# Fewer dense and more listed up blocks in two PEER layers, an earlier end of gate placing, and one gate product per pair of blocks on GpSimd

## The chip, the cores and the metric

The kernel runs on one core of a Trainium2 chip. The engines are TensorE (PE; its weight loads are shown apart as PEld), VectorE (DVE), ScalarE (ACT), GpSimd (POOL) and the queue that issues most DMAs (SP). The metric is the device time of one execution in microseconds; less is better. A difference of 0.2% (some 3 us) is about what a measurement of this kernel can tell from none.

## The reference, cut to what matters

Two layers, each an attention mixer followed by a PEER expert mixer, over 256 tokens of width 1024 in float32. The change touches the PEER mixers alone:

```python
expert = jnp.take_along_axis(cand_idx, pos, axis=-1)   # 8 heads x 16 experts of 16384 for each token
gate = jax.nn.softmax(best, axis=-1)
u = w_down[e_blk]
a = jnp.einsum('td,ted->te', x_blk, u)
hg = jax.nn.gelu(a, approximate=False) * g_blk
y = jnp.einsum('te,ted->td', hg, w_up[e_blk])
```

A token picks 128 of 16384 experts, and y is the sum of their up rows, weighted by gelu times gate.

## The kernel before, in words

**Arithmetic.** A float32 operand is split into two float16 parts, high and low, and a product is three matmuls: high by high, high by low, low by high (`mm3`, `proj`, `rows`; all are issued at L480).

**The weight stream.** All weights pass through one `Stream`, in blocks of 128 x 1024 float32 (512 KB). SP loads a block into one of 6 `raw` buffers (L212), ACT writes the high part `hi` (L152), DVE the low part `lo` (L161); 6 buffers each of `hi` and `lo` lie between them and PE. Each engine works through its instructions in a fixed order, so what stands behind a waiting instruction waits too.

**The down stage of a PEER layer.** The 16384 experts are laid out as 128 blocks of 128 rows. The activation of every expert for every token is computed: 128 down blocks, taken in 64 pairs, 48 matmuls `d` of 128x256 for a pair (loop at L1576). The gelu goes to `A`, an area of the `arena` with 256 columns (the tokens) for each block (L1587, L1589).

**Placing the gates.** Once the experts are chosen, their gates are placed, in 64 groups of 4 tokens. For a group, `prepare` makes a one-hot matrix `hot` on DVE (L1392), the product `gate` of one-hot and gate, on DVE in the kernel before (L1394), and a second part of `gate` on ACT (four instructions, L1400). A pair of blocks later `place` runs on PE, behind the pair's `d`: eight matmuls `G` and four matmuls `seen` for a group. `G` is then copied by ACT to the blocks of `A` that have not been computed (L1419) and multiplied by DVE into those that have (L1421); a pair that is computed later has its gelu multiplied in by DVE (L1590). Four buffers hold `hot` and `gate`, three PSUM banks hold `G`. How many groups a pair prepares (`want`, L1597) is what is left, shared over the pairs until `END` blocks ahead of the stage's end, and rounded up:

```python
left = max(1, (NKEYS - (END if short else 4) - b0) // 2)
want = min(64 - groups, -(-(64 - groups) // left))
```

With END = 6 and placing begun at block 58, the pairs prepare 1, 2, 3 and then 2 groups each, 32 pairs in all; the last group is placed behind blocks 122 and 123.

**What `seen` is for.** `seen` tells, for each expert outside of the dense blocks, whether a token of the first half (128 tokens) or of the second picks it. From it `lists` (L1424 on) makes, for each of the 128 partitions, a list of the blocks that it needs: JB entries for both halves, JO for each half alone, and what does not fit there is spread over a tail of TB entries. This is a generator: each `list_on(1)` lets it emit one step, three steps per pair at the end of the down stage and one per up item. Its steps for the tail need small matmuls `moved` (L1513), 16 for each 8 columns of ROWTAIL.

**The table.** In DRAM lies a `table` for each layer, with one row for each expert outside of the dense blocks: its up row, copied there block by block during earlier stages (L217), and its 256 activations, stored from `A` by SP in three parts of the tokens as they are complete (`store`, L1545).

**The up stage.** `ITEMS` sets the order: first the DENSE up blocks, which are loaded straight from the input, then the listed blocks, each a gather of 128 table rows by a GpSimd DMA (L208) into one of 9 places that lie over the last blocks of `A`. A block for both halves takes 12 matmuls `y` of 128x512, a block for one half takes 6. `xh` and `xl` are the split activations of an item, `hi` and `lo` its split weights. A gather may start only when all stores and copies into the table have landed.

**A flag.** If the lists do not hold all that the tokens need, the program computes everything again without lists.

Of the kernel before, what the change touches and what calls it, by code (L numbers as in the profile page):

```python
# [65 lines left out]
LEAST, MOST, ROW, SMALL = 64.0, 2.0 ** 40, 4.0, 2.0 ** -24  # L66
BOTH, MOSTLY = 128, 1120
CHECKS = 7 * P
DENSE, HEAD = 20, 20
RARE = P - DENSE  # L70
JB, JO, TB, ROWTAIL = 32, 24, 16, 32
BOTHS = JB + TB
WIDE = D + T
PARTS = (0, 128), (128, 192), (192, 256)
FETCHED, DEEP = 9, 8
LISTED = BOTHS + 2 * JO
END = 6
CHUNKED = 4
TO_PE, FROM_PE, TAIL_READY = 3, 4, 42

# [254 lines left out]
def tile_trunk(ctx: ExitStack, tc: tile.TileContext, ins, out: bass.AP, short, shared):  # L335
    nc = tc.nc
# [19 lines left out]
    def ps(name):  # L356
        return psp.tile([P, 512], F32, tag="ps", name=name)
# [115 lines left out]
    def dve(emit):  # L473
        return link("dve", emit)
# [16 lines left out]
    def proj(o, blk, w=P, late=False):  # L491

        h, l = blk
        if late:
            for c in range(NC):
                mm(o, h[:, c * w : (c + 1) * w], xh[:, c, :], c == 0, False)
                mm(o, h[:, c * w : (c + 1) * w], xl[:, c, :], False, False)
            for c in range(NC):
                ins = mm(o, l[:, c * w : (c + 1) * w], xh[:, c, :], False, c == NC - 1)
            return ins  # L500
        for c in range(NC):
            s = slice(c * w, (c + 1) * w)
            ins = mm3(o, (h[:, s], l[:, s]), (xh[:, c, :], xl[:, c, :]), c == 0, c == NC - 1)
        return ins
# [690 lines left out]
    def peer(li):  # L1195
# [165 lines left out]
        def spend(income):  # L1361

            purse[0] += income
            while purse[0] > 0:
                cost = next(bg, None)
                if cost is None:
                    return True
                purse[0] -= cost
            return False
# [15 lines left out]
        def prepare(g4, engine):  # L1385
            hot = ohp.tile([P, 2, P, 4], F16, tag="V", name="hot")
            gate = ohp.tile([P, 2, 4, P], F16, tag="U", name="gate")
            four = slice(4 * g4, 4 * g4 + 4)
            with ExitStack() as order:
                if short and 0 < g4 < 4:  # L1390
                    order.enter_context(tc.issue_after(begun["gate"]))
                nc.vector.tensor_tensor(hot, iota4[:, None].to_broadcast([P, 2, P, 4]),  # L1392
                                        place16[:, :, None, four].to_broadcast([P, 2, P, 4]), op=ALU.is_equal)
            ins = engine.tensor_tensor(gate[:, 0], hot[:, 1].rearrange("p c j -> p j c"),  # L1394
                                       gate16[:, four, None].to_broadcast([P, 4, P]), op=ALU.mult)
            if g4 == 0:
                begun["gate"] = ins.ins
            for j in range(4):
                t = 4 * g4 + j
                nc.scalar.mul(gate[:, 1, j, :], hot[:, 1, :, j], rest[:, t : t + 1])  # L1400
            onehot[g4] = hot, gate

        def place(g4, done):

            p = py(g4 % (3 if short else 4), f"G{g4}")
            if short and g4 == 0:
                begun["seen"] = py(3, "seen")
            hot, gate = onehot.pop(g4)
            for j in range(4):
                for i in range(2):  # L1410
                    mm(p[:, j * P : (j + 1) * P], hot[:, 0, :, j], gate[:, i, j, :], i == 0, i == 1)
                    if short and i == 0:
                        h, k = divmod(4 * g4 + j, P)
                        mm(begun["seen"][:, h * RARE : (h + 1) * RARE], hot[:, 0, :, j], gate[:, 0, j, DENSE:], k == 0,
                           k == P - 1)
            pv = p.rearrange("p (t b) -> p b t", b=P)
            tsl = slice(4 * g4, 4 * g4 + 4)
            if done < P:
                nc.scalar.mul(A[:, done:, tsl], pv[:, done:, :], 1.0 / GSCALE)  # L1419
            if done:  # L1420
                nc.vector.scalar_tensor_tensor(A[:, :done, tsl], pv[:, :done, :], 1.0 / GSCALE, A[:, :done, tsl],  # L1421
                                               op0=ALU.mult, op1=ALU.mult)
# [114 lines left out]
        def store(part, upto):  # L1537

            b0 = stored[part]
            b1 = min(b0 + CHUNKED, NKEYS)  # L1540
            if b0 < b1 <= upto:
                ts = slice(*PARTS[part])
                cols = slice(D + ts.start, D + ts.stop)
                rows_of = table[li][(b0 - DENSE) * P : (b1 - DENSE) * P, cols].rearrange("(b a) t -> a b t", a=P)
                nc.sync.dma_start(rows_of, A[:, b0:b1, ts])  # L1545
                stored[part] = b1
# [3 lines left out]
        def list_on(n):  # L1550
            for _ in range(n):
                next(listing[0], None)
# [3 lines left out]
        def cut(n):  # L1556
            if n >= len(PAIRED):
                return
            i = PAIRED[n]
            k, slot = ITEMS[i][1], slice(SLOTS[i], SLOTS[i] + 2)  # L1560
            hh, al = xh[:, slot, :], xl[:, slot, :]
            if n == 0:
                four = spare16.rearrange("p (a b) -> p a b", b=T)
                hh, al = four[:, 0:2, :], four[:, 2:4, :]
            total = split.total("most")
            act(lambda: split.high(hh, A[:, k : k + 2, :], A_UNIT))
            dve(lambda: split.low(al, A[:, k : k + 2, :], A_UNIT, hh, total))
            for j in range(2):
                made[i + j] = hh[:, j, :], al[:, j, :]
# [4 lines left out]
        groups = prepared = 0  # L1574
        ready = False
        for b0 in range(0, NKEYS, 2):  # L1576
            p = ps(f"d{b0}")
            pv = p.rearrange("p (j t) -> p j t", t=T)
            chosen = ready
            for j in range(2):  # L1580
                proj(pv[:, j, :], ws.get())
                ready = ready or spend(PACE)
            if b0 == 0:
                chains["pe"] = None
            t0 = 4 * groups
            if t0 < T:
                nc.scalar.activation(A[:, b0 : b0 + 2, t0:], pv[:, :, t0:], AF.Gelu, scale=1.0 / unit)  # L1587
            if t0 > 0:
                nc.scalar.activation(pv[:, :, :t0], pv[:, :, :t0], AF.Gelu, scale=1.0 / unit)  # L1589
                dve(lambda: nc.vector.tensor_tensor(A[:, b0 : b0 + 2, :t0], A[:, b0 : b0 + 2, :t0], pv[:, :, :t0],  # L1590
                                                    op=ALU.mult))
            while groups < prepared:
                place(groups, b0 + 2)
                groups += 1
            if chosen:
                left = max(1, (NKEYS - (END if short else 4) - b0) // 2)
                want = min(64 - groups, -(-(64 - groups) // left))  # L1597
                assert want <= 3, b0
                for _ in range(min(want, 1 + groups)):
                    prepare(prepared, nc.gpsimd if want == 1 else nc.vector)  # L1600
                    prepared += 1
            if short:
                for part, (_, upto) in enumerate(PARTS):
                    if 4 * groups >= upto:
                        for _ in range(3 if part == len(PARTS) - 1 else 2):
                            store(part, b0)
                if groups == 64:
                    if listing[0] is None:
                        chains["dve"] = None
                        cut(0)  # L1610
                        listing[0] = lists()
                    if b0 < NKEYS - 2:
                        list_on(3)
# [135 lines left out]

    mla()  # L1750
    peer(0)
    dsa()
    return peer(1)


# [91 lines left out]
```

## Time and profile before

| | |
|---|---|
| median of 3 runs | 1566.35 us (1565.62 to 1566.42) |
| the profiled execution | 1568.7 us |
| its span | 1566.8 us |
| granted PE clock | 0.997 |
| PE busy | 1544.2 us (99%) |
| DVE busy | 1360.7 us (87%) |
| ACT busy | 1080.4 us (69%) |
| POOL busy | 390.9 us (25%) |
| DMA | 313 GB/s mean |

A row of a timeline reads: start and duration in us, engine, line, operation, tile written and tiles read, shape, count, and in brackets how long the engine sat idle before it and what released it. A row of the windows view reads: the stretch, its length, the busy time (and instruction count) of PE, PEld, DVE, ACT and POOL, then the granted clock, the share of the DMA engines and GB/s. A row of the chain of waits reads: start, duration, engine, what. In the group view of a window the two numbers behind the bar are busy time and the mean duration in ns; instructions overlap at their ends, so the busy time divided by the count is what one costs in a row. The first layer's up stage begins at 517.4 us and the second's at 1311.1 us; the text calls either moment E.

### The profile page before, as it was taken

The page shows a single profiled execution, that of the slowest core. Times are in us where ns is not written, and L with a number is a line of the kernel's source. Part 1 is how long each engine was busy: PE and PEld are TensorE (multiplying, and loading weights), DVE is VectorE, ACT ScalarE, POOL GpSimd, SP SyncE. Part 2 cuts the span into 40 slices and gives each one's busy share as a digit, 9 for nine tenths or more (in the row PEclk, how much of TensorE's full clock was granted, in tenths as well). Part 3 has the DMA queues.
Part 4 walks back from the last instruction along what each step waited for, and adds up shares of the span by engine and source line. Part 5 has one row for each costly group of instructions (what it writes and reads, how often), then busy time and mean ns, then how long its engine had stood idle before and what let it go on. Part 6 is the DMA issues. An engine that isn't in the chain of part 4 may idle for free.

```text
span 1566.8 us, 33568 instructions
## 1 busy us (share of the span) xinstructions
PE 1544.2 (99%) x12275; PEld 1136.4 (73%) x12275; DVE 1360.7 (87%) x3815; ACT 1080.4 (69%) x1968; POOL 390.9 (25%) x330
## 2 busy tenths in 40 slices
PE   9999999999999999999999999999999999999996
PEld 7769888899999544444578698888999996444443
DVE  8689999999998879888798699989999997698885
ACT  7667657698887547667578675655988884567673
POOL 3002243200000136654022112344000000366540
PEclk9999999999999999999999999999999999999998
DMA  9999888999877999998599977888988798799992
GB/s 366 391 345 338 299 303 289 361 410 344 285 235 219 308 333 381 364 370 300 192 418 369 375 271 272 289 285 319 379 305 275 257 262 225 287 318 386 389 339 82
DMA packets 207246, 491.09 MB, mean 313 GB/s; under 512 B 71392, under 2 KB 100320, under 8 KB 207072
## 3 DMA queue, kind: packets, MB, share of 16 engines
q1 hardware_dynamic: 177984, 358.31, 64.8%
q0 software_dynamic: 28800, 130.04, 22.1%
q8 instruction: 98, 1.61, 0.4%
q14 instruction: 76, 0.62, 0.1%
q10 hardware_dynamic: 288, 0.52, 0.1%
HBM read 456.03 MB, written 147.06 MB: 385 GB/s over the span
## 4 chain that ended last, share of the span: by engine, by line
PE 90%; DVE 6%; issue 2%; ACT 1%; DMA 0%; POOL 0%; DVEq 0%; POOLq 0%; ACTq 0%
PE d L480 36%; PE y L480 32%; PE pq L480 4%; PE G L480 4%; DVE lo L161 3%; PE q L480 3%; PE v L480 2%; PE seen L480 2%; PE qw L480 1%; PE s L480 1%; PE ps L480 1%; PE h L480 1%; PE qi L480 1%; DVE arena L1314 1%; PE o L480 1%
## 5 line engine op out<-in xcount | busy, mean ns | idle before, releaser
L480 PE MATMUL d<-xh,lo 128*128 128x256 f16 x2048 | 558.3, 273 | 2.3 <-DVE lo L161 2.1
L480 PE MATMUL d<-xl,hi 128*128 128x256 f16 x2048 | 558.2, 273 | 0.0
L480 PE MATMUL d<-xh,hi 128*128 128x256 f16 x2048 | 558.2, 273 | 0.0
L480 PEld LDWEIGHTS <-hi 128*128 128x128 f16 x5016 | 488.6, 98 | 57.5 <-issue 0.9
L161 DVE SCALAR_TENSOR_TENSOR lo<-raw,hi 128x1024 f16<-128x1024 f32 (+1 forms) x359 | 452.2, 1267 | 66.8 <-ACT hi L152 64.4
L152 ACT ACTIVATE hi<-raw 128x1024 f16<-128x1024 f32 (+1 forms) x355 | 367.8, 1048 | 147.5 <-PE d L480 69.4
L208 POOL DMA_INDIRECT arena<-table,up_at x160 | 180.9, 1131 | 655.0 <-DMA raw<-in_up 499.7
L480 PEld LDWEIGHTS <-xh 128*128 128x128 f16 x1712 | 166.2, 98 | 199.8 <-issue 3.5
L161 DVE SCALAR_TENSOR_TENSOR lo<-arena,hi 128x512 f16<-128x512 f32 (+1 forms) x382 | 258.6, 713 | 46.5 <-ACT hi L152 44.7
L480 PEld LDWEIGHTS <-lo 128*128 128x128 f16 x2508 | 245.7, 98 | 33.3 <-DVE lo L161 4.4
L152 ACT ACTIVATE hi<-arena 128x1024 f16<-128x1024 f32 x200 | 208.5, 1052 | 51.1 <-issue 23.1
L480 PE MATMUL y<-lo,xh 128*128 128x512 f16 x784 | 237.1, 379 | 0.8 <-DVE lo L161 0.5
L480 PE MATMUL y<-hi,xh 128*128 128x512 f16 x784 | 235.6, 379 | 2.1 <-ACT hi L152 2.1
L480 PE MATMUL y<-hi,xl 128*128 128x512 f16 x784 | 235.7, 379 | 0.0
L1400 ACT ACTIVATE gate<-hot,rest 128x128 f16<-128x128 f16 x512 | 168.4, 405 | 15.2 <-DVE hot L1392 13.1
L152 ACT ACTIVATE xh<-arena 128x256 f16<-128x256 f32 (+2 forms) x214 | 85.7, 406 | 112.3 <-PE y L480 76.4
L480 PEld LDWEIGHTS <-xl 128*128 128x128 f16 x856 | 83.1, 98 | 104.0 <-DVE xl L161 4.3
L262 POOL TENSOR_TENSOR lo<-raw,hi 128x1024 f16<-128x1024 f32 x26 | 60.6, 2330 | 186.7 <-ACT hi L260 160.1
L1392 DVE TENSOR_TENSOR hot<-iota,place 128x1024 f16<-128x1024 f16 x128 | 87.8, 687 | 15.8 <-PE G L480 15.5
L480 PE MATMUL G<-gate,hot 128*128 128x128 f16 x1024 | 92.3, 219 | 1.0 <-DVE arena L1421 1.0
L480 PEld LDWEIGHTS <-hot 128*128 128x128 f16 x1536 | 89.1, 113 | 2.5 <-issue 1.2
L161 DVE SCALAR_TENSOR_TENSOR xl<-arena,xh 128x256 f16<-128x256 f32 (+2 forms) x216 | 88.5, 417 | 2.4 <-ACT xh L152 2.1
(270 smaller groups left out, 1841.5 us busy)
## 6 DMA issues: line engine op xcount, KB each, us to landing
raw<-in_down SPq DMA_DIRECT2D x256, 512.0 KB, 5.2
table<-in_up SPq DMA_DIRECT2D x218, 512.0 KB, 6.9
raw<-in_up SPq DMA_DIRECT2D x40, 512.0 KB, 6.1
table<-arena SPq DMA_DIRECT2D x110, 128.0 KB, 3.9
table<-arena SPq DMA_DIRECT2D x54, 256.0 KB, 4.9
raw<-in_peer_q SPq DMA_DIRECT2D x24, 512.0 KB, 10.0
raw<-in_dsa_qk SPq DMA_DIRECT2D x16, 512.0 KB, 10.4
raw<-in_mla_w_o SPq DMA_DIRECT2D x8, 512.0 KB, 9.8
```

The lines of the kernel that those rows point to most:

```text
L152: return nc.scalar.copy(o, src) if unit == 1.0 else nc.scalar.mul(o, src, unit)
L161: return nc.vector.scalar_tensor_tensor(o, src, unit, hi, op0=ALU.mult, op1=ALU.subtract, accum_out=total)
L208: self.fetched = self.nc.gpsimd.indirect_dma_start(t, None, table, bass.IndirectOffsetOnAxis(ap=at, axis=0)).ins
L262: nc.gpsimd.tensor_tensor(lo, raw, hi if short else hi.bitcast(F32), op=ALU.subtract)
L480: return pe(lambda: nc.tensor.matmul(o, l, r, start=start, stop=stop, skip_group_check=True))
L1314: dve(lambda: nc.vector.tensor_reduce(exp_[t][:, h - 1, :], held, axis=AX.X, op=ALU.add))
L1392: nc.vector.tensor_tensor(hot, iota4[:, None].to_broadcast([P, 2, P, 4]), place16[:, :, None, four].to_broadcast([P, 2, P, 4]), op=ALU.is_ ...
L1400: nc.scalar.mul(gate[:, 1, j, :], hot[:, 1, :, j], rest[:, t : t + 1])
```

## The change

DENSE goes from 20 to 14, and the tail list from 16 to 20 entries a partition (with 40 instead of 32 candidates), so the listed blocks go from 96 to 100: 52 for both halves instead of 48, and 48 for one half as before. With HEAD, which stays equal to DENSE, the stores must end six items into the up stage earlier. END goes from 6 to 12. In the short program, a pair with more than 4 groups placed gives the first of its gate products to GpSimd; the others stay on DVE.

```diff
-DENSE, HEAD = 20, 20
+DENSE, HEAD = 14, 14
 RARE = P - DENSE
-JB, JO, TB, ROWTAIL = 32, 24, 16, 32
+JB, JO, TB, ROWTAIL = 32, 24, 20, 40
 ...
-END = 6
+END = 12
 ...
-                for _ in range(min(want, 1 + groups)):
-                    prepare(prepared, nc.gpsimd if want == 1 else nc.vector)
+                for first in [True, False, False][: min(want, 1 + groups)]:
+                    prepare(prepared, nc.gpsimd if want == 1 or short and first and groups > 4 else nc.vector)
```

By the rule for `want`, the pairs now prepare 1, 2, seven times 3 and twenty times 2 groups, 29 pairs in all, and the last group is placed behind blocks 116 and 117. 26 gate products a layer go to GpSimd and 38 stay on DVE. The other constants follow: RARE goes from 108 to 114, so `seen` is 114 columns wide, and 115 instead of 109 blocks are copied to each table.

First place: DVE in the down stage of the first layer, around blocks 90 to 92, where a pair prepares two groups. `lo135` and `lo136` are low parts of later weight blocks, `hot` and `gate` belong to two groups, `G` to the groups just placed, and `d90` is the pair's gelu. Before:

```order
L161 SCALAR_TENSOR_TENSOR lo135_5773,sums_94<-raw135_5520,hi135_5772 128x1024
L1392 TENSOR_TENSOR hot_5835<-iota4_106,place16_102 128x1024
L161 SCALAR_TENSOR_TENSOR lo136_5855,sums_94<-raw136_5551,hi136_5854 128x1024
L1392 TENSOR_TENSOR hot_5843<-iota4_106,place16_102 128x1024
L1394 TENSOR_TENSOR gate_5836<-hot_5835,gate16_103 128x512
L1421 SCALAR_TENSOR_TENSOR arena_65<-G30_5693,arena_65 128x92x4
L1421 SCALAR_TENSOR_TENSOR arena_65<-G31_5708,arena_65 128x92x4
L1590 TENSOR_TENSOR arena_65<-arena_65,d90_5627 128x2x120
L1394 TENSOR_TENSOR gate_5844<-hot_5843,gate16_103 128x512
```

The same pair in the changed kernel:

```order
L161 SCALAR_TENSOR_TENSOR lo135_5923,sums_94<-raw135_5667,hi135_5922 128x1024
L1392 TENSOR_TENSOR hot_5985<-iota4_106,place16_102 128x1024
L161 SCALAR_TENSOR_TENSOR lo136_6005,sums_94<-raw136_5699,hi136_6004 128x1024
L1392 TENSOR_TENSOR hot_5993<-iota4_106,place16_102 128x1024
L1421 SCALAR_TENSOR_TENSOR arena_65<-G36_5843,arena_65 128x92x4
L1590 TENSOR_TENSOR arena_65<-arena_65,d90_5777 128x2x144
L1421 SCALAR_TENSOR_TENSOR arena_65<-G37_5858,arena_65 128x92x4
L1394 TENSOR_TENSOR gate_5994<-hot_5993,gate16_103 128x512
```

One L1394 is gone from DVE's pair, the one whose `hot` is made first; it stands on POOL now, between that engine's last reductions of expert numbers and its first gathers, where nothing stood. Six more groups have been placed by the same pair (G36 in place of G30).

Second place: ACT at the end of the first layer's dense head. In the kernel before, up block 19, the last dense one, is weight block 186, and `hi187` from the arena is the first listed one; the short `xh` rows are activations of listed items. Before:

```order
L152 ACTIVATE hi184_8013<-raw184_7951 128x1024
L152 ACTIVATE xh_100<-arena_65 128x256 x2
L152 ACTIVATE hi185_8032<-raw185_7979 128x1024
L152 ACTIVATE xh_100<-arena_65 128x128
L152 ACTIVATE xh_100<-arena_65 128x256
L152 ACTIVATE hi186_8057<-raw186_7997 128x1024
L152 ACTIVATE hi187_8075<-arena_65 128x1024
```

In the changed kernel the last dense block is up block 13, weight block 180:

```order
L152 ACTIVATE hi178_7912<-raw178_7855 128x1024
L152 ACTIVATE hi179_7929<-raw179_7876 128x1024
L152 ACTIVATE hi180_7954<-raw180_7896 128x1024
L152 ACTIVATE hi181_7980<-arena_65 128x1024
L152 ACTIVATE xh_100<-arena_65 128x256
L152 ACTIVATE hi182_8003<-arena_65 128x1024
```

No listed item's activation stands ahead of a dense block's high part any more; it is so in the second layer too.

Third place: SP at the first layer's turn to the up stage, from its last stores on (`128x4x64` is a store of the third part of the tokens, for four blocks). Before, `raw177` is up block 10:

```order
L212 DMA raw176_7721<-in_up 128x1024
L1545 DMA table0_119<-arena_65 128x4x64 x3
L212 DMA raw177_7746<-in_up 128x1024
L1545 DMA table0_119<-arena_65 128x4x64 x3
L212 DMA raw178_7769<-in_up 128x1024
```

In the changed kernel `raw175` is up block 8:

```order
L212 DMA raw174_7695<-in_up 128x1024
L212 DMA raw175_7739<-in_up 128x1024
L1545 DMA table0_119<-arena_65 128x2x128
L1545 DMA table0_119<-arena_65 128x2x64 x2
L212 DMA raw176_7805<-in_up 128x1024
```

The last store stands ahead of the load of up block 9 now, and ahead of that of up block 11 before.

## Prediction

> **What bounds the kernel now.** I read the page first, then the chain of waits, then the busy time by stretch.
>
> ```profile
> PE 1544.2 (99%) x12275; PEld 1136.4 (73%) x12275; DVE 1360.7 (87%) x3815; ACT 1080.4 (69%) x1968; POOL 390.9 (25%) x330
> PE 90%; DVE 6%; issue 2%; ACT 1%; DMA 0%; POOL 0%; DVEq 0%; POOLq 0%; ACTq 0%
> ```
>
> By stretch:
>
> ```profile
> 303.00:340.00 37.00, 36.52 (x408) 33.47 (x409) 35.36 (x68) 35.73 (x93) 0.00 (x0) 1.00 1.03 417
> 310.00:505.00 195.00, 194.52 (x2149) 178.48 (x2147) 180.76 (x331) 164.00 (x422) 0.00 (x0) 1.00 0.89 307
> 440.00:480.00 40.00, 40.00 (x448) 36.77 (x447) 38.36 (x67) 32.51 (x85) 0.00 (x0) 1.00 0.77 215
> 510.00:570.00 60.00, 58.55 (x305) 29.56 (x304) 43.56 (x130) 28.94 (x39) 12.04 (x9) 1.00 1.01 341
> 1304.00:1364.00 60.00, 58.55 (x303) 29.36 (x302) 43.60 (x130) 28.82 (x39) 10.48 (x9) 1.00 0.90 297
> 594.00:760.00 166.00, 166.00 (x771) 75.26 (x770) 139.06 (x509) 113.02 (x167) 85.01 (x82) 1.00 0.87 328
> ```
>
> PE is busy all the time and carries the chain. In the stretch where gates are placed (310 to 505) PE rests 0.48 us, in the listed part of the up stage (594 to 760) never, and at the turn between them (510 to 570, and 1304 to 1364 in the second layer) 1.45 us. So a change here is worth what it takes off PE's own work, less the waits that it makes. DVE is the next engine: 180.76 of 195 us while gates are placed, 38.36 of 40 late in that stretch. POOL does nothing there.
>
> **Less work on PE: the up blocks.** The chain gives the length of a block.
>
> ```profile
> 324.56 5.24 PE d L480 x48
> 331.08 5.24 PE d L480 x48
> 500.43 5.24 PE d L480 x48
> 506.94 10.48 PE d L480 x96
> 517.42 38.85 PE y L480 x180
> ```
>
> 180 matmuls `y` take 38.85 us, 0.216 each, so an up block for all tokens (12) is 2.59 us and one for half of them 1.30. Before, a layer has 20 + 48 + 48/2 = 92 full blocks' worth, afterwards 14 + 52 + 24 = 90. Two layers save four: **-10.4 us**.
>
> **More work on PE.** `seen` grows from 108 to 114 columns, and the tail list from four rounds of 16 `moved` to five.
>
> ```profile
> 309.20 0.21 PE L480 MATMUL seen<-gate,hot 128*128 128x108 f16 x1
> ...
> 309.36 0.21 PE L480 MATMUL seen<-gate,hot 128*128 128x108 f16 x1
> ...
> 585.87 0.17 PE L1513 MATMUL moved<-U,to 128*128 128x16 f16 x1
> ...
> 586.35 0.18 PE L1513 MATMUL moved<-V,to 128*128 128x16 f16 x1
> 586.38 0.59 PE L480 MATMUL y<-hi,xh 128*128 128x512 f16 x2
> ```
>
> From one `seen` to the next, with two `G` of 128 columns between, are 0.16 us: 364 columns at 0.43 ns, nearly the 0.42 ns of `y` (0.216 us for 512). Six more columns are 2.5 ns, and there are 512 such matmuls: **+1.3 us** (0 if short matmuls have a floor). A round of `moved` holds PE from 585.87 to 586.38; one more in each layer is **+1.0 us** (at 0.03 us for a matmul of 16 columns, 20 are taken to cost the same). The number of `d` and `G` stays. END moves placing, it does not add to it: three pairs fewer carry the same 64 groups, so these pairs are longer (5.24 us, and 6.51 - 5.24 = 1.27 for two groups, so 0.64 a group) and the last ones shorter.
>
> **The turn to the up stage.** PE's waits there have names, and they are the same in both layers.
>
> ```profile
> 566.31 0.42 ACT L152 ACTIVATE xh<-arena 128x256 f16<-128x256 f32 x1 [2.79 <-PE y L480]
> 566.63 1.04 ACT L152 ACTIVATE hi<-raw 128x1024 f16<-128x1024 f32 x1
> ...
> 567.72 0.59 PE L480 MATMUL y<-hi,xh 128*128 128x512 f16 x2 [1.07 <-ACT hi L152]
> 569.07 0.38 PE L480 MATMUL y<-lo,xh 128*128 128x512 f16 x1 [0.24 <-DVE lo L161]
> ...
> 1361.37 0.59 PE L480 MATMUL y<-hi,xh 128*128 128x512 f16 x2 [1.07 <-ACT hi L152]
> 1362.71 0.38 PE L480 MATMUL y<-lo,xh 128*128 128x512 f16 x1 [0.24 <-DVE lo L161]
> ```
>
> ACT sits on a listed item's activation, which waits for PE to free its slot, and the high part of the last dense block stands behind it; PE then waits 1.07 + 0.24 us. In the changed order no listed activation stands ahead of a dense high part. I take the wait as gone in both layers, **-2.6 us**, with 0 as the other end. What is late next there is the first gather, and that is a rival below.
>
> **Placing: the GpSimd product.** Four costs, by engine. *PE* loses nothing of its own. *ACT*: three groups in a pair instead of two, seven times a layer instead of once.
>
> ```profile
> 316.62 0.22 PE L480 MATMUL G<-gate,hot 128*128 128x128 f16 x1 [0.48 <-DVE arena L1421]
> ...
> 318.80 0.55 ACT L1587 ACTIVATE arena<-d 128x488 f32<-128x488 f32 x1
> 325.94 0.53 ACT L1587 ACTIVATE arena<-d 128x464 f32<-128x464 f32 x1
> 331.73 0.52 ACT L1587 ACTIVATE arena<-d 128x448 f32<-128x448 f32 x1
> ```
>
> The kernel before has one such pair; ACT's round there is 325.94 - 318.80 = 7.14 us, PE's is 5.24 + 3 x 0.64 = 7.15, so ACT keeps step, and with two groups its round is 5.79. PE's one wait of that pair, 0.48 us for a PSUM bank that DVE had not emptied, follows a burst of first products and stays. If each of the six further pairs had it too, that would be 6 us for both layers; I take 0, since DVE is then relieved.
>
> *DVE and POOL* are the uncertain part. What a product costs on DVE and what POOL does to DVE:
>
> ```profile
> L1394 DVE TENSOR_TENSOR gate<-hot,gate 128x512 f16<-128x512 f16 x60 | 40.9, 682 | 0.0
> L1421 DVE SCALAR_TENSOR_TENSOR arena<-G,arena 128x264 f32<-128x264 f32 (+30 forms) x62 | 31.9, 532 | 0.5 <-ACT arena L1419 0.5
> ...
> 280.90 1.70 POOL L1310 TENSOR_TENSOR arena<-arena 128x800 f32<-128x800 f16 x1 [1.58 <-DVE arena L1307]
> ...
> 254.41 2.13 POOL L262 TENSOR_TENSOR lo<-raw,hi 128x1024 f16<-128x1024 f32 x1 [8.15 <-ACT hi L260]
> ...
> 255.38 2.24 DVE L161 SCALAR_TENSOR_TENSOR lo<-raw,hi 128x1024 f16<-128x1024 f32 x1
> 257.55 0.08 DVE L161 DVE_READ_ACCUMULATOR lo<-raw,hi 128x1 f32 x1
> ...
> 262.04 1.22 DVE L161 SCALAR_TENSOR_TENSOR lo<-raw,hi 128x1024 f16<-128x1024 f32 x1
> ```
>
> A product holds DVE 0.68 us; 26 fewer in a layer free some 17 us of it. POOL needs 1.70 us for 800 elements and 2.13 for 1024, so about 1.1 for 512, once a pair: far from full, and the product is the group that is made first, used a round later. Were it late, PE would stand at `G` with the next pair's `d` behind it. But the `lo` that began at 255.38, while POOL worked until 256.54, took 2.24 us instead of 1.22: DVE stood still until POOL was done. At worst a pair loses 1.1 us of DVE for 0.68 saved, +0.4. Late in the stretch DVE has (40 - 38.36) / 6.1 = 0.27 us left in a pair of 6.51, so it would fall 0.15 us behind in each of the last 12 pairs, 1.8 us a layer. At best the product runs beside L1421 and L1590, and nothing is lost; no gain is possible where PE rests 0.48 us. I take 0.75 a layer, **+1.5 us**.
>
> The Trainium skill, "SBUF — State Buffer", Who interferes with whom, has a rule that speaks against this edit: DVE and GpSimd share one pair of ports, a DVE instruction with two SBUF inputs and a GpSimd one that reads SBUF exclude each other for their whole length, and one with a single SBUF input is free. The 2.24 us agrees with it. By it `lo`, `hot` and `gate` are blocked, but not L1421 and L1590, which read PSUM; no run here shows that last part yet. If every product fell beside these two the sum would be -10.7, and if each fell on the others -7.1.
>
> **What else moves.** Lists begin three pairs earlier, where pairs have no placing, and DVE has room there (PE 5.24 us a pair, two `lo` 2.4). 12 more blocks are copied to tables, 12 fewer loaded straight, 8 more gathered: the copies fall on 303 to 390, where the DMA engines are full already (share 1.03) and PE still worked 36.52 of 37. I cost these at 0; the gathers run under 166.00 of 166 us of PE.
>
> **The sum.** -10.4 + 1.3 + 1.0 - 2.6 + 1.5 = -9.2 us: the profiled execution of 1568.7 us would take 1559.5. The median is 2.35 us below it; I keep that distance: 1566.35 - 9.2 = **1557.2 us**. With every unknown at its good end (seen 0, placing 0) it is 1554.4, with every one at its bad end (turn 0, placing +6 and +3.6) 1567.9.
>
> **Rivals.** *First: DVE loses the whole product.* If DVE's gaps in a pair are not free (they are waits for `hi` and for `G`) and POOL also falls on `lo` or `hot` each time, each of the 52 products holds up the round by its full 1.1 us, the saved 0.68 only widening gaps: 57 us, and the time is 1566.35 - 10.7 + 57 = 1613; half of it gives 1584. It turns slower when a product costs PE over 0.26 us on average (13.8 / 52: the 10.7 us of all other terms, and 3.1 for the 0.2%). For it: DVE at 92% and the blocked `lo`. Against: PE has two to three blocks of split weights ahead, and `gate` from POOL is due a round later. The page of the Trainium skill named above would have it so for `lo` and `hot`. Chance 0.12.
>
> *Second: the first gathers come late.* The dense head that covers lists, stores and first gathers shrinks by 6 x 2.59 = 15.5 us.
>
> ```profile
> 532.69 1.75 SPq L1545 DMA_DIRECT2D table<-arena  x3
> ...
> 539.97 1.77 POOL L208 DMA_INDIRECT arena<-table,up_at  x1 [250.23 <-DMA raw<-in_up]
> ...
> 563.21 0.31 ACT L152 ACTIVATE xh<-arena 128x128 f16<-128x128 f32 x1 [0.72 <-DMA arena<-table,up_at]
> ```
>
> Now the last stores go out at E + 17, the first gather at E + 22.6, and the sixth has landed at E + 45.8; its item begins at E + 62.2. Afterwards that item begins at E + 14 x 2.59 + 10.4 = 46.7. The stores now stand two loads earlier in SP's order, and the last placing ends five pairs ahead of E, 26 us, instead of two, 10.5; I expect the first gather near E + 13, and the sixth landed at E + 36. If the stores went out no earlier, it would land at E + 45.8, and with 4 us to split it the stage would wait 3 us a layer: 1557.2 + 6 = 1563, within 0.2%. Chance 0.13.
>
> *Third: the lists don't hold.* By the reference's own picks the tail needs 2357 and 2433 entries in the two layers, of 20 x 128 = 2560; 16 x 128 would not do. If the flag fell all the same, the time would more than double. Chance 0.01.
>
> **How the numbers follow.** The forecast has 0.74; nine tenths of it lie below 1563.2, the bound of faster by 0.2%, the rest within 0.2% of before. With the rivals: faster 0.70, same 0.16, slower 0.14. The forecast's own range is 1554.4 to 1567.9; the range given is 1554 to 1567, which takes in the second rival and leaves out the first, the third and the ends.
>
> **What would show it.** In the profile after: `y` shorter by 48 matmuls; no wait of 1.07 us on `hi` at the turn; placing rounds of 7.15 and 6.51 us with PE at 100%; first gathers near E + 13. A PE wait on `gate`, on L1421 or on `lo` in the placing rounds shows the first rival, one on `hi` from the arena after the dense head the second. The forecast is wrong if PE's idle time while gates are placed grows by more than 7 us in both layers together.

## The result, and the profile after

The changed kernel takes 1558.51 us (median of 5 runs, 1557.95 to 1559.19) beside 1566.42 us of the kernel before (5 runs): a ratio of 0.9948, 95% interval 0.9937 to 0.9958. That is 7.9 us less, more than the 0.2% that a measurement can tell from none. The profiled execution is the median run, with a span of 1556.6 us and a granted clock of 0.998.

From the page, the busy times and the shares of the chain of waits that ended last:

```profile
PE 1534.9 (99%) x12259; PEld 1134.8 (73%) x12259; DVE 1358.8 (87%) x3781; ACT 1075.4 (69%) x1963; POOL 493.4 (32%) x391
PE 73%; DVE 11%; DMA 5%; ACT 5%; issue 4%; SPq 1%; DVEq 0%; POOL 0%; ACTq 0%; POOLq 0%
```

PE works 9.3 us less. The chain ran through PE for 90% of the span before; now DVE, ACT and DMAs carry a fifth of it. By stretch (length, then busy time of PE, PEld, DVE, ACT, POOL, clock, DMA share, GB/s):

```profile
303.00:340.00 37.00, 35.97 (x408) 32.91 (x406) 35.33 (x67) 36.14 (x96) 4.80 (x4) 1.00 1.03 417
310.00:505.00 195.00, 193.56 (x2148) 177.35 (x2147) 180.26 (x319) 163.69 (x423) 45.55 (x26) 1.00 0.93 319
440.00:480.00 40.00, 39.73 (x435) 36.19 (x434) 36.85 (x61) 32.09 (x84) 11.11 (x7) 1.00 0.88 250
510.00:570.00 60.00, 60.00 (x358) 32.65 (x356) 50.17 (x150) 30.95 (x41) 19.16 (x16) 1.00 1.02 363
1304.00:1364.00 60.00, 60.00 (x356) 30.43 (x354) 50.39 (x155) 34.55 (x50) 22.02 (x19) 1.00 0.93 327
```

At the turn PE now never rests (60.00 of 60, 58.55 before). While gates are placed it rests 1.44 us of 195 (0.48 before), and late in that stretch, where it never rested, it works 39.73 of 40, although DVE has less to do (36.85 of 40 us, before 38.36).

PE's waits among the first pairs of three groups, from its timeline:

```profile
317.67 0.22 PE L480 MATMUL G<-gate,hot 128*128 128x128 f16 x1 [0.44 <-DVE arena L1421]
326.25 0.22 PE L480 MATMUL G<-gate,hot 128*128 128x128 f16 x1 [0.59 <-DVE arena L1421]
```

The first stood before too (0.48 us); the second is new. Its cause stands in the rows of DVE and POOL just ahead of it:

```profile
324.24 1.06 POOL L1394 TENSOR_TENSOR gate<-hot,gate 128x512 f16<-128x512 f16 x1 [6.05 <-DVE hot L1392]
324.42 0.17 DVE L1590 TENSOR_TENSOR arena<-arena,d 128x24 f32<-128x24 f32 x1
324.51 1.34 DVE L1394 TENSOR_TENSOR gate<-hot,gate 128x512 f16<-128x512 f16 x1
325.77 0.42 DVE L1421 SCALAR_TENSOR_TENSOR arena<-G,arena 128x264 f32<-128x264 f32 x1
```

While POOL makes its product, DVE's own product takes 1.34 us instead of 0.68, and the L1421 that empties a PSUM bank comes late. In a pair of two groups the rows of the two engines look so:

```profile
430.66 0.69 DVE L1392 TENSOR_TENSOR hot<-iota,place 128x1024 f16<-128x1024 f16 x1
431.27 1.22 DVE L161 SCALAR_TENSOR_TENSOR lo<-raw,hi 128x1024 f16<-128x1024 f32 x1
431.43 1.96 POOL L1394 TENSOR_TENSOR gate<-hot,gate 128x512 f16<-128x512 f16 x1 [6.01 <-DVE hot L1392]
432.41 0.08 DVE L161 DVE_READ_ACCUMULATOR lo<-raw,hi 128x1 f32 x1
432.41 1.53 DVE L1392 TENSOR_TENSOR hot<-iota,place 128x1024 f16<-128x1024 f16 x1
433.86 0.55 DVE L1421 SCALAR_TENSOR_TENSOR arena<-G,arena 128x392 f32<-128x392 f32 x1
```

The product is due when the first `hot` is done, but `lo` has begun by then; it stands still until `lo` ends (1.96 us where the one above took 1.06), and then the second `hot` stands still until the product ends: 1.53 us instead of 0.69. The chain of waits shows what this costs, one round from `hot` to `hot` (the view leaves out short pieces; the 1.01 us of "issue" lie in the `lo` that begins at 436.28):

```profile
430.75 0.60 DVE hot L1392
431.35 1.14 DVE lo L161 x2
432.50 1.45 DVE hot L1392
434.09 0.21 issue
434.29 1.01 ACT gate L1400 x3
435.30 0.96 ACT hi L152
436.43 1.01 issue
437.52 0.60 DVE hot L1392
```

The second `hot` releases ACT's four L1400, behind these stands ACT's next `hi`, and behind `hi` DVE's next `lo` and `hot`. This loop takes 437.52 - 430.75 = 6.77 us, PE's own round 6.53. Without the 0.84 us it would be 5.93, shorter than PE's round.

How this reaches PE is seen at `G`, in the pair shown above:

```profile
433.95 0.28 PE L480 MATMUL G<-gate,hot 128*128 128x128 f16 x2
434.11 0.57 PE L480 MATMUL G<-gate,hot 128*128 128x128 f16 x2
```

Two `G` take 0.28 us in the first row and 0.57 in the second. The late one, at 434.47, is the first of the pair's second group. It writes the PSUM bank of three groups before, which L1421 empties, and that L1421 stands behind the second `hot` and ends at 433.86 + 0.55 = 434.41. In the traces the time from the end of this L1421 to that `G` shrinks by some 0.25 us a round: 2.1, 1.9, 1.6 and so on to 0.4, then 0.05. From there on PE waits; five rounds in each layer take 6.6 to 6.8 us. Then L1421 comes ahead of the second `hot`:

```profile
459.51 0.59 DVE L1421 SCALAR_TENSOR_TENSOR arena<-G,arena 128x424 f32<-128x424 f32 x1
460.03 1.02 DVE L1392 TENSOR_TENSOR hot<-iota,place 128x1024 f16<-128x1024 f16 x1
```

The bank is free 1.2 us ahead of its `G`, and PE is back at 6.53 us, although DVE's rounds still take 6.77 up to the last pair.

### The profile page after: what moved, and what is told of

The parts are those of the page before. It is cut to its first block, busy times and chain, and to the rows that moved or that the text cites. A ratio compares the mean times of both kernels' runs of the same rounds, so it can differ in the third digit from the quotient of the medians.

```text
span 1556.6 us, 33639 instructions
## 1 busy us (share of the span) xinstructions
PE 1534.9 (99%) x12259; PEld 1134.8 (73%) x12259; DVE 1358.8 (87%) x3781; ACT 1075.4 (69%) x1963; POOL 493.4 (32%) x391
## 4 chain that ended last, share of the span: by engine, by line
PE 73%; DVE 11%; DMA 5%; ACT 5%; issue 4%; SPq 1%; DVEq 0%; POOL 0%; ACTq 0%; POOLq 0%
PE y L480 32%; PE d L480 22%; DVE lo L161 5%; PE pq L480 4%; PE q L480 3%; DVE hot L1392 3%; DMA raw<-in_down 3%; ACT hi L152 2%; DMA table<-in_up 2%; ACT gate L1400 2%; PE v L480 2%; PE G L480 2%; PE qw L480 1%; PE s L480 1%; PE ps L480 1%
## 5 line engine op out<-in xcount | busy, mean ns | idle before, releaser
L161 DVE SCALAR_TENSOR_TENSOR lo<-raw,hi 128x1024 f16<-128x1024 f32 (+1 forms) x346 | 443.2, 1290 | 59.4 <-ACT hi L152 58.0
L152 ACT ACTIVATE hi<-raw 128x1024 f16<-128x1024 f32 (+1 forms) x342 | 350.4, 1046 | 111.9 <-DMA raw<-in_down 29.5
L161 DVE SCALAR_TENSOR_TENSOR lo<-arena,hi 128x512 f16<-128x512 f32 (+1 forms) x398 | 269.4, 714 | 65.7 <-ACT hi L152 64.9
L152 ACT ACTIVATE hi<-arena 128x1024 f16<-128x1024 f32 x208 | 218.5, 1055 | 98.3 <-issue 63.2
L480 PE MATMUL y<-lo,xh 128*128 128x512 f16 x768 | 231.2, 379 | 0.0
L480 PE MATMUL y<-hi,xl 128*128 128x512 f16 x768 | 230.8, 379 | 0.0
L480 PE MATMUL y<-hi,xh 128*128 128x512 f16 x768 | 230.8, 379 | 0.0
L1400 ACT ACTIVATE gate<-hot,rest 128x128 f16<-128x128 f16 x512 | 169.5, 402 | 50.4 <-DVE hot L1392 48.1
L1394 POOL TENSOR_TENSOR gate<-hot,gate 128x512 f16<-128x512 f16 x52 | 92.0, 1770 | 301.4 <-DVE hot L1392 301.4
L262 POOL TENSOR_TENSOR lo<-raw,hi 128x1024 f16<-128x1024 f32 x27 | 64.8, 2399 | 197.7 <-ACT hi L260 159.2
L1392 DVE TENSOR_TENSOR hot<-iota,place 128x1024 f16<-128x1024 f16 x128 | 111.9, 876 | 0.1
```

The lines of the kernel that those rows point to most:

```text
L152: return nc.scalar.copy(o, src) if unit == 1.0 else nc.scalar.mul(o, src, unit)
L161: return nc.vector.scalar_tensor_tensor(o, src, unit, hi, op0=ALU.mult, op1=ALU.subtract, accum_out=total)
L262: nc.gpsimd.tensor_tensor(lo, raw, hi if short else hi.bitcast(F32), op=ALU.subtract)
L480: return pe(lambda: nc.tensor.matmul(o, l, r, start=start, stop=stop, skip_group_check=True))
```

## The experiments

Two theories of the placing loss stood at the start. *Port*: the loss is that loop, made by the second `hot` behind the GpSimd product. *Relief*: pairs of three groups are what costs, and the product on GpSimd is what keeps them bearable. A third, *late gate*, came up on the way: PE loses because a gate from GpSimd is ready later. For the turn the theories were *order* (ACT's order decides the wait) and *gathers* (the time of the first gather does).

All stages are taken from the first matmul of a kind to the first of the next, in us; placing runs from the first `G` to the first `y`, the up stage from there to the first `v`, in the second layer to the last matmul.

| kernel | median, us | ratio to before (95%) | placing, layer 1 and 2 | up stage, layer 1 and 2 |
|---|---|---|---|---|
| before_again | 1566.55 (one run) | | 213.67, 214.35 | 243.97, 243.33 |
| changed | 1558.51 | 0.9948 (0.9937 to 0.9958) | 216.92, 216.79 | 236.88, 236.03 |
| dve_products | 1556.01 | 0.9942 (0.9928 to 0.9956) | 215.05, 215.03 | 236.89, 236.05 |
| pool_only | 1577.44 | 1.0069 (1.0056 to 1.0082) | 219.56, 219.51 | 244.00, 243.81 |
| pool_last_before | 1567.77 | 1.0005 (0.9996 to 1.0014) | 215.24, 214.67 | 244.00, 243.50 |
| pool_last | 1553.35 | 0.9914 (0.9901 to 0.9928) | 214.53, 215.15 | 236.86, 236.06 |
| pool_in_threes | 1556.84 | 0.9935 (0.9921 to 0.9948) | 215.71, 215.71 | 236.89, 236.53 |
| end_only | 1561.95 | 0.9973 (0.9963 to 0.9983) | 213.67, 214.56 | 241.45, 240.67 |
| end_8 | 1571.05 | 1.0027 (1.0017 to 1.0038) | 214.03, 214.47 | 245.71, 244.92 |
| lists_only | 1558.61 | 0.9951 (0.9938 to 0.9964) | 215.23, 214.94 | 238.99, 236.05 |

**All products back on DVE (dve_products).**

```diff
-                    prepare(prepared, nc.gpsimd if want == 1 or short and first and groups > 4 else nc.vector)
+                    prepare(prepared, nc.gpsimd if want == 1 else nc.vector)
```

> The changed kernel, with every gate product of the placing pairs back on DVE (14 dense blocks, END 12 stay). Theory 'port': the cost of the GpSimd product is that DVE's second hot waits for it (1.53 us instead of 0.69), which makes a loop hot - high part on ACT - lo of 6.77 us out of a round of 6.53; without it the five rounds of 6.8 us late in each layer go back to 6.53 (-2.4 us in all), hot has 0.69 everywhere. The pairs of three groups then have three products on DVE, which was busy 7.18 of 7.18 us in the changed kernel, 0.48 of it a lo that stood still: 7.18 - 0.48 + 0.60 = 7.30 a round, six rounds a layer, +1.4 us. Together 1557.5 us, 1556 to 1559. Theory 'relief' (the rival: the product on GpSimd is what makes pairs of three possible, and the lost time comes from three groups in a pair): DVE needs the whole 0.68 us more in each of the 12 pairs of three, +8 us, 1566.5, with PE waiting for G or for gates there.

Placing falls by 1.87 and 1.76 us, the late rounds are 6.53 again, and the time is 1556.01 us. *Relief* is out: with three products in a pair DVE keeps the pace, and the rounds have the same 7.18 us, not the 7.30 that I had expected. One of the stretches above in this kernel:

```profile
440.00:480.00 40.00, 40.00 (x442) 36.73 (x440) 39.40 (x70) 32.59 (x86) 0.00 (x0) 1.00 0.93 270
```

Late in placing DVE is busy 39.40 of 40 us and PE never waits; in the changed kernel DVE was busy 36.85 and PE waited. The busy share of DVE says little here; what counts is how long the loop through it is. The times alone do not tell the two kernels apart, as the intervals of their ratios overlap (0.9928 to 0.9956 and 0.9937 to 0.9958); the 3.6 us rest on the traces, in which placing repeats within 0.1 us a layer (dve_products_again: 215.03 and 215.12).

**The product alone (pool_only).** The kernel before, with the new two lines in the loop and its own constants.

```diff
-DENSE, HEAD = 14, 14
+DENSE, HEAD = 20, 20
-JB, JO, TB, ROWTAIL = 32, 24, 20, 40
+JB, JO, TB, ROWTAIL = 32, 24, 16, 32
-END = 12
+END = 6
```

> The kernel before (20 dense blocks, END 6) with the GpSimd product alone added. Theory 'port': from pair 66 to pair 106, some 20 rounds, the second hot stands behind the GpSimd product and the loop takes 6.77 us; PE's lead at the start covers about 1.4 us, so 20 x 0.25 - 1.4 = 3.6 us a layer are lost: 1566.4 + 7.2 = 1573.6 us, 1571 to 1576; from pair 108 on, where L1421 stands between lo and the second hot, rounds have 6.51 again. Theory 'relief': DVE has 0.68 us less in each pair, no round grows, 1566.4 us, 1565 to 1567.

1577.44 us, 11 more than before: eighteen rounds a layer of 6.77 to 6.80 us instead of 6.51, all before the pair from which L1421 stands between `lo` and the second `hot`. PE waits in them at `G` for L1421, as above. The loss is larger than the 7.2 that I worked out: the time in hand at the banks was 0.85 us, not 1.4, and a round loses 0.28, not 0.25. With END 6 the product is a plain loss; in the changed kernel 13 rounds with the second `hot` in that place come before L1421 moves ahead, not 22, and five of them show at PE.

**The same, but the last group's product (pool_last_before).**

```diff
-                for first in [True, False, False][: min(want, 1 + groups)]:
+                for first in [False, False, True][3 - min(want, 1 + groups) :]:
```

> The kernel before with the product of a pair's last group on GpSimd, where pool_only (1577.4 us) had that of the first. DVE's order is the same but for the product left out: lo, hot, lo, hot, gate, L1421, L1421 instead of gate, lo, hot, lo, hot, L1421, L1421. Theory 'port': the product now starts when the second hot has ended; what stands behind it on DVE is, from pair 92 on, L1421, which reads one operand from PSUM and runs beside it, and up to pair 90 the other group's gate, which waits for up to 1.04 us, but at the end of DVE's round and not inside the loop hot - high part - lo. Rounds stay at 6.51: 1566.4 us, 1565 to 1568, no hot of 1.53 us. Theory 'late gate' (the rival: PE loses since a gate from GpSimd is ready later, 1.97 us instead of 0.68 after its hot): now it is the last gate of the pair that is late, a whole hot later than before, so rounds grow as much or more, 1577 or more, with PE's waits at G.

1567.77 us, not told apart from before; the rounds of two groups take 6.51 us but for one of 6.8. The gate is ready later than in pool_only, and 9.7 us are gone (9.2 of them in placing, by the traces): *late gate* is out, *port* holds.

**The changed kernel with the last group's product (pool_last, pool_last_again), beside dve_products_again.** The diff is the one above.

> The changed kernel (14 dense blocks, END 12) with the product of a pair's last group on GpSimd instead of the first. Theory 'port': the five rounds of 6.8 us in each layer go back to 6.53; in the pairs of three the product stands beside L1590 and then the next gate, as costly as now. So placing takes what dve_products took (215.0 us) to 1 us more a layer: 1556 to 1558 us. Theory 'late gate': 1558.5 or more, with PE's waits at G.

> The changed kernel with the last group's product on GpSimd once more (1553.35 us before), beside the kernel with all products on DVE (1556.0 us) on the same chip. By the traces placing and the up stage take 902.6 us here and 903.0 there, so the two should not differ by over 1 us: 1554 to 1556 both. If a DVE with room (0.68 us less a pair) takes up disturbances that PE otherwise feels, this one stays 2 us or more ahead.

> The changed kernel with every product on DVE once more, for the comparison on the same chip: 1554 to 1556 us by the traces' stages; 1556 or more if the product on GpSimd is worth something of its own.

1553.35 us the first time. On one chip the two kernels then took 1555.58 us (0.9925, 0.9912 to 0.9939) and 1556.26 us (0.9927, 0.9913 to 0.9940): the same. The lead of the first time is not to be relied on. Both beat the kernel before and, by the traces' placing (430.3 and 430.2 us for both layers in these two runs, 433.7 in the changed kernel), the changed one; a product on GpSimd, even where it hurts nobody, brings nothing that can be measured over DVE. A pair of pool_last, on DVE and POOL:

```profile
427.51 0.68 DVE L1392 TENSOR_TENSOR hot<-iota,place 128x1024 f16<-128x1024 f16 x1
428.11 0.55 DVE L1421 SCALAR_TENSOR_TENSOR arena<-G,arena 128x392 f32<-128x392 f32 x1
428.33 1.04 POOL L1394 TENSOR_TENSOR gate<-hot,gate 128x512 f16<-128x512 f16 x1 [5.05 <-DVE hot L1392]
428.59 1.34 DVE L1394 TENSOR_TENSOR gate<-hot,gate 128x512 f16<-128x512 f16 x1
```

The product runs its 1.04 us at once. L1421, which reads `G` from PSUM, takes its usual 0.55 us beside it; `gate`, which reads two SBUF operands, takes 1.34 instead of 0.68, but at the end of DVE's round, where the loop doesn't pass.

**The product in pairs of three only (pool_in_threes).**

```diff
-                    prepare(prepared, nc.gpsimd if want == 1 or short and first and groups > 4 else nc.vector)
+                    prepare(prepared, nc.gpsimd if want == 1 or short and first and groups > 4 and want > 2 else nc.vector)
```

> The changed kernel with the GpSimd product in the pairs of three groups alone. Theory 'port': the five rounds of 6.8 us go (they belong to pairs of two), the longer round of the second pair of three (7.93 us, where dve_products had 7.26) stays: placing 215.7 us a layer, 1556.8 us. Theory 'late gate' or a cost of the pairs of three alone: as the changed kernel, 1558.5.

1556.84 us; the second bank wait (0.58 us) and its round of 7.92 us are there, the rounds of 6.8 are not, and placing takes 215.71 us in both layers. So of the 1.8 us that the product costs in a layer 0.7 are that bank wait and 1.1 to 1.2 the late rounds.

**END alone (end_only).**

```diff
-END = 6
+END = 12
```

> The kernel before (20 dense blocks, all products on DVE) with END 12 alone. Both theories: no y matmul goes, and the wait of 1.07 us on the high part at the turn stays, since the order of the up stage's items hangs on the number of dense blocks and not on when lists begin. Theory 'port': the pairs of three groups cost the second bank wait (0.59 us a layer) and 0.1 a round of DVE: 1566.4 + 1.2 + 1.4 = 1569.0, 1567 to 1570. Theory 'relief': +8 us for the products that DVE then lacks room for, 1574. If the wait at the turn goes here (it hung on late gathers, against my prediction's reason), the time falls by up to 5 us from these.

This expectation failed on the turn. Placing costs nothing more, as before_again shows, but the up stage is 2.5 and 2.7 us shorter without a block less: END 12 takes the turn's waits away with 20 dense blocks as well. ACT there:

```profile
556.71 0.42 ACT L152 ACTIVATE xh<-arena 128x256 f16<-128x256 f32 x1 [2.12 <-PE y L480]
557.04 1.04 ACT L152 ACTIVATE hi<-raw 128x1024 f16<-128x1024 f32 x1
559.35 0.42 ACT L152 ACTIVATE xh<-arena 128x256 f16<-128x256 f32 x1 [1.28 <-issue]
559.67 1.04 ACT L152 ACTIVATE hi<-raw 128x1024 f16<-128x1024 f32 x1
560.62 0.29 ACT L152 ACTIVATE xh<-arena 128x128 f16<-128x128 f32 x1
560.82 1.04 ACT L152 ACTIVATE hi<-raw 128x1024 f16<-128x1024 f32 x1
...
565.01 0.42 ACT L152 ACTIVATE xh<-arena 128x256 f16<-128x256 f32 x1 [1.12 <-PE y L480]
```

The last dense `hi` (560.82) is done before the listed `xh` of 256 columns that waits for PE (565.01); in the kernel before it stood behind that one. It is still ACT's order, but END moves it too. END also brings the first gather from E + 22.7 to E + 14.9 us (E: start of the up stage), so the time of the gathers could be the cause as well. That is what the next kernel is for.

**END 8 alone (end_8).**

```diff
-END = 6
+END = 8
```

> The kernel before (20 dense blocks, products on DVE) with END 8 instead of 6: placing ends one pair earlier than in the kernel before. In ACT's order the last two high parts of dense blocks then stand behind a listed item's activation of 128 columns; with END 6 the last one stands behind one of 256 columns that waits 2.79 us for PE. Theory 'order': that is enough, the waits of 1.07, 0.24 us and those behind them at the turn go in both layers as with END 12, 1562 us, 1561 to 1564 (end_only: 1561.95). Theory 'early gathers': END 12 took the waits away because the first gather came at E + 14.9 instead of E + 22.7 us; with END 8 it comes near E + 20, so most of the wait stays: 1565 us or more.

1571.05 us: both expectations missed, since the waits grew. The first gathers come earlier than before (E + 18.9 and E + 18.5), so *gathers* is out. PE's and ACT's rows:

```profile
561.53 0.59 PE L480 MATMUL y<-hi,xh 128*128 128x512 f16 x2 [1.07 <-ACT hi L152]
562.80 0.59 PE L480 MATMUL y<-lo,xh 128*128 128x512 f16 x2 [0.68 <-DVE lo L161]
566.08 0.38 PE L480 MATMUL y<-lo,xh 128*128 128x512 f16 x1 [0.24 <-DVE lo L161]
568.00 0.61 PE L480 MATMUL y<-hi,xl 128*128 128x512 f16 x2 [1.54 <-DVE xl L161]
```

```profile
557.48 0.42 ACT L152 ACTIVATE xh<-arena 128x256 f16<-128x256 f32 x1 [1.18 <-PE y L480]
560.11 0.42 ACT L152 ACTIVATE xh<-arena 128x256 f16<-128x256 f32 x1 [2.22 <-PE y L480]
560.44 1.04 ACT L152 ACTIVATE hi<-raw 128x1024 f16<-128x1024 f32 x1
```

I had counted the last dense `hi` alone; here it is the third last, behind two listed activations in a row. The three kernels fit together once these are counted. A listed activation can't run before PE has freed its slot, and the fifth one comes at the same time in all: E + 43.9 in end_8 (560.11, E = 516.24), in end_only (559.35, E = 515.48) and in the kernel before (E = 517.25 by the first `y`):

```profile
561.13 0.42 ACT L152 ACTIVATE xh<-arena 128x256 f16<-128x256 f32 x1 [2.22 <-PE y L480]
```

What differs is which dense `hi` stands right behind the fifth. PE wants block n at E + 2.59 n. In the kernel before it is block 18 (wanted at E + 46.6: in time), and two more listed ones stand ahead of block 19 (wanted at E + 49.2, made at 566.63, E + 49.4: late). With END 8 it is block 17, wanted at E + 44.0: late, and so is what follows on DVE. With END 12 block 17 stands behind the fourth and block 19 ahead of the seventh: nothing is late.

**The lists alone (lists_only).** 14 dense blocks, END 6, no product on GpSimd; so that the stores end in time, up to seven instead of three of the last part go out at a time. Against the changed kernel, with the line of dve_products besides:

```diff
-END = 12
+END = 6
-                        for _ in range(3 if part == len(PARTS) - 1 else 2):
+                        for _ in range(7 if part == len(PARTS) - 1 else 2):
```

> 14 dense blocks and 100 listed ones alone: END 6, all products on DVE; the last third of the table is stored in bursts of up to seven DMAs a pair instead of three, as 14 dense blocks leave more to store after placing. Theory 'order' (the turn's gain comes from the order of the items): the four blocks' y -10.4, seen +1.3, moved +1.0, the waits at the turn -5.3 and no loss in placing: 1566.4 - 13.4 = 1553.0 us, 1552 to 1555, faster than the changed kernel. Theory 'gathers' (my second rival): with lists three pairs later and a dense head that is 15.5 us shorter the first gathers come too late, PE waits 3 us or more a layer for the high part of gathered blocks: 1559 or more.

1558.61 us, between the two. Here, too, the 1.07 us on `hi` are gone, so 14 dense blocks alone do that as well. The first gathers go out at E + 24.7 and E + 24.9, the latest of all kernels, and PE then loses 2.1 us in the first layer, in waits like this one for `lo`, and nothing in the second (236.05 us, as in dve_products):

```profile
574.36 0.38 PE L480 MATMUL y<-lo,xh 128*128 128x512 f16 x1 [0.23 <-DVE lo L161]
```

My second rival had its conditions in this kernel and gave a third of its price. Why only the first layer pays is open. The expected 1553 was too low anyway: dve_products, which has the same terms without these waits, takes 1556.

**The kernel before once more (before_again).** No edit.

> The kernel before, unchanged, for a second profile: the first one's execution took 1568.7 us, 2.35 over the median, and I compared stages against it. If the 2.35 us lie in the choosing stages (which the change does not touch), placing and the up stage show 214.4 and 243.5 to 244.0 us again, and the differences by stage hold as they are; if they lie in placing or the up stage, my account of the turn (-5.2 us) holds too much.

It took 1566.55 us. The 2.15 us that it is faster lie mostly ahead of the first `d` (0.50), in the choosing stages (330.64 instead of 331.53 us in both layers) and in one wait of 0.65 us at the first pair of three groups, which comes in some executions and not in others. Over all profiles the choosing stages, which nothing here touches, take 329.4 to 332.6 us. The account of the turn holds.

## Why the prediction was right, point by point

*The up blocks*, -10.4 us: right. *The up stage* as a whole is 7.09 and 7.30 us shorter than in before_again; 5.18 are the 24 matmuls `y` fewer in a layer at 0.216.

*`seen`*, +1.3: right. Rounds went from 6.51 to 6.53 (and from 7.15 in end_only to 7.18 with three groups), 20 x 0.02 + 7 x 0.03 = 0.6 a layer; short matmuls have no floor there. *`moved`*, +1.0: right. The first and the last row of a round in the changed kernel, with 0.03 us more to the last one's end, make 0.53 us for 16:

```profile
569.33 0.17 PE L1513 MATMUL moved<-U,to 128*128 128x20 f16 x1
...
569.83 0.18 PE L1513 MATMUL moved<-V,to 128*128 128x20 f16 x1
```

*The turn*, -2.6: the step "In the changed order no listed activation stands ahead of a dense high part. I take the wait as gone in both layers" is right (with 14 dense blocks, and END 12 would have done it too), its size was half. It measured 7.09 + 7.30 - 10.4 + 1.0 = 5.0 us. I had added up what stands in brackets, 1.07 + 0.24. Two costs have no bracket. A bracket counts from the end of the record before it, and in a row the next matmul starts ahead of that end: in the kernel before, the two `y` at 566.06 end by their record at 566.65, and 1.07 on that is 567.72, but without a wait the next would have started at 566.06 + 2 x 0.216 = 566.49, so 1.23 us were lost. And a wait for weights shows on PEld, not on PE:

```profile
566.06 0.59 PE L480 MATMUL y<-hi,xl 128*128 128x512 f16 x2
...
579.21 0.74 PE L480 MATMUL y<-lo,xh 128*128 128x512 f16 x2
579.92 0.60 PE L480 MATMUL y<-hi,xl 128*128 128x512 f16 x2
```

```profile
579.91 0.11 PEld L480 LDWEIGHTS <-xl 128*128 128x128 f16 x2 [0.60 <-DVE xl L161]
```

Two `y` take 0.43 us; from 579.21 to 579.92 are 0.71, and PE shows no idle time. From start to start, less 0.216 for each `y`, the turn lost 1.23 + 0.30 + 0.39 + 0.28 + 0.32 = 2.5 us in a layer.

*Placing*, +1.5: the cause was half right, the size too small. dve_products puts the product at 1.87 + 1.76 = 3.6 us, the end of my range for DVE alone. I had named the blocking, but charged it to DVE's spare time in a pair ("Late in the stretch DVE has (40 - 38.36) / 6.1 = 0.27 us left in a pair of 6.51, so it would fall 0.15 us behind"). What decides is not that spare time but the loop `hi`, `lo`, `hot`, L1400, `hi`: 5.93 us, with 0.60 of slack, into which 0.84 fell. DVE then slips 0.25 us a round against PE, and PE feels it where L1421 empties a bank too late. The lead in split blocks, on which the prediction counted, held: PE lost nothing at `d`. And the bank wait, which I had as likely not to come again ("I take 0, since DVE is then relieved"), came once more in each layer, since DVE's product beside POOL's takes longer, not shorter.

The Trainium skill, "SBUF — State Buffer", Who interferes with whom, says that a DVE instruction with two SBUF inputs and a GpSimd one that reads SBUF exclude each other, that whichever comes first holds the ports to its end, and that one SBUF input is free. The runs agree in all three: `hot` 1.53 and `gate` 1.34 us behind the product, the product 1.96 behind `lo`, and L1421 0.55 beside it. The last part, which no trace of before had shown, also shows its worth in pool_only: PE's rounds go from 6.78 back to 6.51 us in the pair from which L1421 stands between `lo` and the second `hot` and runs while POOL does. DVE's rounds stay at 6.78 there, so what helps PE is the earlier bank, not a shorter loop.

*What I had at 0*: END's longer pairs cost nothing (end_only), nor do the copies to tables: the 1.03 us that PE rests from 303 to 340 are the two bank waits, 0.44 + 0.59. The first gathers came at E + 15.9 and E + 15.7 instead of E + 13, early enough.

The sum becomes -10.4 + 1.3 + 1.0 - 5.0 + 3.6 = -9.5 where the prediction had -9.2: two terms were off by over 2 us each, with opposite signs, and that they cancel is luck. Against the median of 7.9 (6.6 to 9.9 by the interval) both fit.

## What to carry to other kernels

When work goes from DVE to GpSimd, look at what DVE does in the instant in which that work becomes due: an instruction with two SBUF inputs will stand still for it, one that reads PSUM will not, and the wait hurts only if it lies inside a loop of engines with less slack than the wait, however idle DVE is on average. Then find what that loop releases for the busiest engine: here one L1421 moved one place ahead hid the loss. Count PE's losses from start to start; what stands in brackets left out half of those at the turn. A wait that hangs on the order of one engine's queue can jump when any constant that shifts this order is moved, so such a constant is worth trying at several values: END 6, 8 and 12 gave 1566, 1571 and 1562 us with all else equal.

## What the runs showed of the hardware that was not expected

GpSimd took its turn between two DVE instructions that were both ready: the product waited from 431.43 until `lo` ended at 432.41, and the next `hot`, which stood in DVE's queue and follows `lo` at once in dve_products, began to work only after it. In pool_only the second `hot` stands still in this way in 22 rounds of each layer. A stretch of DVE that is "busy" holds such standing still: in the pairs of three groups from 338 to 366.7 us DVE is busy 28.70 of 28.70 us both in the changed kernel, where it makes two products a pair, and in dve_products, where it makes three at the same pace.

```profile
L161 DVE SCALAR_TENSOR_TENSOR lo<-raw,hi 128x1024 f16<-128x1024 f32 x8 | 11.7, 1457 | 0.0
```

```profile
L161 DVE SCALAR_TENSOR_TENSOR lo<-raw,hi 128x1024 f16<-128x1024 f32 x8 | 9.7, 1217 | 0.0
```

These are the groups of `lo` in that stretch, of the changed kernel and of dve_products: 1457 ns on average in the first, 1217 in the second. The difference in the mean of the same instruction, not the busy share, gives the blocking away.
